# Attention's value products as one 64-column sum, with a tile of its own for minima and sums, output tiles allocated later, four buffers moved and a new instruction order

## The chip, the cores and the metric

The kernel runs on one core of a Trainium2 chip. A core has five engines that run their own instruction queues side by side: TensorE (PE, matrix products into PSUM; its weight loads are listed apart as PEld), VectorE (DVE), ScalarE (ACT), GpSimd (POOL) and SyncE (SP, which issues the DMAs here). The metric is the device time of one execution in microseconds; lower is better. Times given are medians of several runs. A profile is one further execution that was recorded.

## What is computed

One step of a decoder layer with two parallel mixers, for a prompt of 2048 tokens and for 8 x 8 sampled tokens, all in float32 at the interface:

```python
h = rmsnorm(x, norm_w)
z = h @ w_in
q, k, v, qb, kb, vb, g_lr, gate_a, gate_b = jnp.split(z, split_points(), axis=-1)
q = rope(rmsnorm(heads(q, H_A), q_norm_w), pos)
k = rope(rmsnorm(heads(k, H_A), k_norm_w), pos)
o_a = attend(q, k, v)                       # 8 heads x 64, three dilated windows
log_a = jax.nn.log_sigmoid(g_lr @ w_gate_up + b_gate) / GATE_TAU
o_b, s_fin = gla_chunked(qb * (DK_B ** -0.5), kb, vb, log_a, s0)   # 4 heads
o_b = rmsnorm(o_b, gla_norm_w)
mixed = jnp.concatenate([o_a * silu(gate_a), o_b * silu(gate_b)], axis=-1)
y = x + mixed @ w_out
```

Attention has three branches, (window, dilation) = (128, 1), (512, 4), (2048, 16). In each, a query sees at most 129 keys of its residue class:

```python
s = jnp.einsum('brnqhd,brnkhd->brnqhk', qr, kk) * (hd ** -0.5)
s = jnp.where(valid, s, -jnp.inf)
m = jnp.max(s, axis=-1, keepdims=True)
p = jnp.exp(s - m)
den = jnp.sum(p, axis=-1)
o = jnp.einsum('brnqhk,brnkhd->brnqhd', p, v) / den[..., None]
lse = m + jnp.log(den)
```

The three outputs are mixed by a softmax over their `lse`. Outputs are y, the new keys and values, and the GLA states.

## The kernel before

Products that need float32 accuracy are made from float16 halves: a number is kept as a high part and a low part, and a product is the sum of high x high, high x low and low x high. Projections (`project`, L1762) do so for each block of weights in w_in: v, q, k first, then qkb, g (in two halves g0, g1), vb and gb, tile by tile of 128 tokens. Their sums go to two PSUM banks (pool `ps_Y`), and ACT or DVE takes each out in `post`.

Attention (`attend`) works in units: 64 units of four heads for branches 1 and 2 (`unit`) and 32 half-blocks of branch 3 (`branch3`). A unit passes four steps, and units follow one another in a pipeline that is woven into the projections:

- `qk`: PE makes the scores (L1031); DVE adds the mask, scales, and takes the negated maximum as a running minimum (L1039); ACT makes the exponential and its sum (L1042). Minimum and sum go to columns 65 and 64 of the unit's output tile `o` (66 numbers a head).
- `tr`: PE transposes the probabilities (L1049), and `split` makes the two halves `pt`. Every other tile is split by ACT and DVE (L1008, L1009). The others are copied by ACT (L1011), copied once more to float16 by ACT or DVE (L1013, L1015), and the low part is POOL's subtraction (L1016). A counter decides which.
- `pv`: the value products (L1065). The values lie as [high | low], 128 columns a head. The high half of `pt` takes all 128 columns in one product, giving two sums side by side; the low half takes the 64 high columns.
- `post`: `added` has ACT copy the second sum to SBUF (`ol`, L1081) and DVE add it to the first (L1082) into `o`; a DMA writes `o` out.

The tile `o` is allocated before the scores, since minimum and sum are written to it, and is held until its DMA has read it. The outputs of the value products share two PSUM banks (`ps_O`) with GLA.

GLA works in chunks of 256 tokens (`gla_core`, `gla_prompt`), `gla_out` normalizes its output, `combine` mixes, and `finish` makes the output projection (L2121). The sampled tokens' long-range scores are multiplied on POOL (`dot`) from the cache tiles k2 and k3.

The tile framework finds the semaphores. The order in which every engine takes its instructions isn't the program's: a table `ORDER` lists, for each engine, the numbers of the traced instructions in the order wanted, and `in_order` (L675) makes each one follow its predecessor in that list. `ACT.preload_act_table_set` (L695) loads the ACT table that serves both Ln and Exp, and it too stands where the list puts it; ahead of it the compiler adds table loads of its own.

Of the kernel before, what the change touches and what calls it, by code (L numbers as in the profile page):

```python
# [7 lines left out]
F32 = mybir.dt.float32  # L8
# [10 lines left out]
P = 128  # L19
D = 1024  # L20
KT = D // P
NH = 8
# [2513 lines left out]
```

## Time and profile before

| what | value |
|---|---|
| median of 3 runs | 1230.56 us (1227.27 to 1232.08) |
| profiled execution | 1224.72 us, its span 1222.9 us |
| granted TensorE clock, mean | 0.995 |
| DVE, ACT, POOL busy | 915.3, 825.3, 540.0 us |
| value products (L1065) | 1200, 157.4 us busy |
| HBM | 183.02 MB read, 75.24 MB written |

In the rows of the profile, L and a number is a line of the kernel before. A group's row gives the engine, the operation, what it writes and reads, shapes, the count, then busy time and the mean of one in ns, then the idle time of the engine just before and what ended it. A row of the list of waits gives who waited for whom, the total in us, the times and the longest. A row of the timeline gives start and length in us; rows of one kind that follow each other are merged, with their count. The stage rows give, for each stretch, the busy time of each engine and, in brackets, its instructions, then the granted clock, the DMA engines' busy share and GB/s. A PE row's length includes the passage through the array, so neighbours overlap: the time that a product holds PE is read from start to next start.

### The profile page before, as it was taken

What the parts mean: (1) busy time and instruction counts of PE and PEld (TensorE: products, weight loads), DVE (VectorE), ACT (ScalarE), POOL (GpSimd) and SP (SyncE); (2) the same over time, 40 slices, a digit from 0 to 9 for tenths busy, and PEclk for the clock granted to TensorE, in tenths of its full rate; (3) what the DMA queues carried; (4) which work ended last, traced back from release to release, by engine and by line L of the source; (5) the groups of instructions that cost most, each with busy time, mean ns of one, the idle gap of its engine ahead of it and who ended that gap; (6) DMA issues with size and microseconds to landing.
All of it is one profiled execution on the core that took longest, in us unless ns stands there. A gap on an engine that the chain in (4) does not pass through costs nothing. (4 is left out here: it accounts for less than half of the span.)

```text
span 1222.9 us, 26121 instructions
## 1 busy us (share of the span) xinstructions
PE 1168.8 (96%) x8942; PEld 704.6 (58%) x8942; DVE 915.3 (75%) x2457; ACT 825.3 (67%) x2189; POOL 540.0 (44%) x478
## 2 busy tenths in 40 slices
PE   3999999999999889998999999999999999999998
PEld 1444465566566556665767676646556666555543
DVE  5888787978878957777778765688889999743562
ACT  7656599789779968997877563677778864521220
POOL 0054344465647335563345467655534454311220
PEclk9899999999999999999999999999999999999999
DMA  7477956777955897799999987856672287999962
GB/s 260 160 234 211 238 194 140 213 217 206 228 174 168 198 262 234 250 233 317 284 237 268 256 243 226 266 167 214 224 234 96 96 271 249 330 374 402 391 218 74
DMA packets 235831, 283.07 MB, mean 231 GB/s; under 512 B 116193, under 2 KB 146866, under 8 KB 232626
## 3 DMA queue, kind: packets, MB, share of 16 engines
q1 hardware_dynamic: 235698, 281.40, 76.1%
q8 instruction: 71, 1.16, 0.4%
q14 instruction: 62, 0.51, 0.1%
HBM read 183.02 MB, written 75.24 MB: 211 GB/s over the span
## 5 line engine op out<-in xcount | busy, mean ns | idle before, releaser
L1617 POOL TENSOR_TENSOR pr<-k,qb 128x512 f32<-128x512 f32 x128 | 169.4, 1324 | 141.9 <-DVE sck L1618 72.8
L1762 PEld LDWEIGHTS <-hr 128*128 128x128 f16 x1824 | 170.5, 98 | 103.9 <-issue 12.4
L1042 ACT ACTIVATE p<-p,o 128x256 f32<-128x256 f32 (+1 forms) x384 | 173.8, 456 | 24.3 <-DVE o L1039 16.8
L2121 PE MATMUL Y<-w_o,mh 128*128 128x512 f16 x768 | 187.7, 379 | 0.2 <-DVE xr L2128 0.2
L1762 PEld LDWEIGHTS <-hl 128*128 128x128 f16 x1248 | 117.6, 99 | 105.5 <-issue 7.5
L1065 PE MATMUL O<-v,pt 128*128 128x128 f16 (+1 forms) x1200 | 157.4, 206 | 5.6 <-POOL pt L1016 1.9
L1016 POOL TENSOR_TENSOR pt<-p,pt 128x512 f16<-128x512 f32 (+1 forms) x80 | 92.1, 1151 | 141.4 <-ACT pt L1013 88.6
L1049 PE MATMUL t<-ident,p 128*128 128x128 f32 x600 | 136.9, 282 | 4.0 <-ACT p L1042 3.5
L1065 PEld LDWEIGHTS <-pt 128*128 128x128 f16 x1200 | 100.9, 99 | 51.6 <-POOL pt L1016 7.2
L1762 PE MATMUL acc_g<-w_g,hr 128*128 128x272 f16 (+1 forms) x768 | 117.7, 276 | 0.5 <-ACT vbs L1404 0.3
L1762 PE MATMUL acc_v<-w_v,hl 128*128 128x512 f16 x384 | 113.1, 385 | 2.0 <-DVE w_v L1286 0.9
L1618 DVE TENSOR_REDUCE sck<-pr 128x8 f32<-128x512 f32 x128 | 87.2, 681 | 37.1 <-POOL pr L1617 36.7
L2121 PEld LDWEIGHTS <-mh 128*128 128x128 f16 x768 | 71.1, 98 | 69.2 <-issue 3.1
L1762 PE MATMUL acc_q<-w_q,hl 128*128 128x512 f16 x384 | 110.3, 379 | 0.0
L1762 PE MATMUL acc_k<-w_k,hl 128*128 128x512 f16 x384 | 109.4, 379 | 0.0
L1031 PE MATMUL s<-kk,qq 128*128 128x256 f16 (+1 forms) x512 | 106.2, 264 | 3.4 <-DVE o L1039 1.6
L1039 DVE CUSTOM_DVE_ANT_0 p<-s,m3w,scl_s 128x128 f32<-128x128 f32 (+1 forms) x256 | 90.7, 395 | 17.6 <-PE s L1031 8.8
L1762 PE MATMUL acc_vb<-w_vb,hr 128*128 128x512 f16 x384 | 102.1, 379 | 0.9 <-DVE so_g L1304 0.9
L1762 PE MATMUL acc_gb<-w_gb,hr 128*128 128x512 f16 x384 | 96.4, 380 | 0.1
L1049 PEld LDWEIGHTS t<-ident,p 128*128 128x128 f32 x600 | 77.9, 141 | 32.2 <-ACT p L1042 12.1
L1762 PE MATMUL acc_qkb<-w_qkb,hr 128*128 128x512 f16 x288 | 84.2, 379 | 0.0
L2163 POOL TENSOR_TENSOR oc<-oc 128x512 f32<-128x512 f32 x32 | 36.3, 1149 | 101.3 <-DVE oc L2156 86.9
(546 smaller groups left out, 2515.1 us busy)
## 6 DMA issues: line engine op xcount, KB each, us to landing
k<-in_cache_k_win SPq DMA_DIRECT2D x104, 256.0 KB
sv_b<-in_cache_v_win SPq DMA_DIRECT2D x24, 1024.0 KB
hr<-h_d SPq DMA_DIRECT2D x44, 512.0 KB
qb<-q_d SPq DMA_DIRECT2D x64, 256.0 KB
oc<-o_d SPq DMA_DIRECT2D x48, 264.0 KB
o_d<-o SPq DMA_DIRECT2D x64, 132.0 KB
x<-in_x_prompt SPq DMA_DIRECT2D x16, 512.0 KB
h_d<-hl SPq DMA_DIRECT2D x16, 512.0 KB
```

Source lines behind the costliest of these rows:

```text
L1016: POOL.tensor_tensor(l, f, h, ALU.subtract)
L1031: PE.matmul(s_ps[:, i * w : (i + 1) * w], q, k, start=(n == 0), stop=(n == len(prods) - 1),)
L1039: DVE.tensor_tensor_reduce(s[:, sl], s_ps[:, sl], mask, neg, BIG, ALU.add, ALU.min, nmf(i))
L1042: ACT.activation(s[:, sl], s[:, sl], AF.Exp, bias=nmf(i), scale=-1.0, accum_out=denf(i))
L1049: PE.transpose(p_ps[:, i * P : (i + 1) * P], t["s"][:, i * P : (i + 1) * P], ident[:])
L1065: PE.matmul(o_[:, d], t["pt"][:, c, (i * nb + b) * P : (i * nb + b + 1) * P], vf(i, b)[:, d], start=(n == 0), stop=(n == 2 * nb - 1),)
L1617: POOL.tensor_tensor(pr[:], kt, qt, ALU.mult)
L1618: DVE.tensor_reduce(out, pr[:].rearrange("p (u k d) -> p u k d", u=2, k=4), AX.X, ALU.add)
L1762: PE.matmul(z, a_[:, k, :], w[:, p_, k, cols], start=(k == 0 and i == 0), stop=(k == KT - 1 and i == 2),)
L2121: PE.matmul(Y[:], a_[:, k, :], w_[:, part, k, :512], start=(i == 0), stop=(i == len(prods) - 1),)
L2163: eng.tensor_tensor(o_[g], o_[g], w[:, g].unsqueeze(2).to_broadcast([P, NH, HD]), ALU.mult)
```

## The change

Five edits, and a new table.

1. `pv` makes, for each head and key block, three products of 64 columns, all summed in the same 64 columns of the bank: high x high, high x low, low x high. One head's output is 64 columns wide, so a unit uses 256 of a bank's 512 columns, not all.
2. `added` becomes `taken`: DVE copies the 256 columns from the bank to `o`, and ACT copies minimum and sum there from their own tile. The counter of `split` no longer jumps at an output.
3. Minima and sums go to a tile `st` of their own (six buffers), and `o` is allocated only in `post`.
4. Other homes: `gla_out` squares into `ob` rather than a tile of its own; `ct` and `tabs` are in the pool `xp`; the copy of vb is in z3 and z4 rather than z2; the cache tile k2 has two buffers.
5. `ORDER` is another table for all five engines: PE has 8619 numbers instead of 8019, DVE 2046 instead of 2014, ACT 1699 instead of 1731, POOL 474 and SP 1055 as before. Hardly a line of it is the same.

```diff
     def gla_out(gt, O, n, row0, tagp):
-        sq = gt.tile([P, 512], F32, name=f"osq_{tagp}", tag="osq")
+        ob = gt.tile([P, 512], F32, name=f"ob_{tagp}", tag="ob", bufs=2)
         ss = gt.tile([P, 4], F32, name=f"oss_{tagp}", tag="oss")
-        ACT.activation(sq[:n], O[:n], AF.Square)
-        DVE.tensor_reduce(ss[:n], sq[:n].rearrange("p (h d) -> p h d", h=4), AX.X, ALU.add)
+        ACT.activation(ob[:n], O[:n], AF.Square)
+        DVE.tensor_reduce(ss[:n], ob[:n].rearrange("p (h d) -> p h d", h=4), AX.X, ALU.add)
...
-                    for n in range(2 * nb):
-                        b, c = divmod(n, 2)
-                        d = slice(0, P - HD * c)
-                        PE.matmul(
-                            o_[:, d], t["pt"][:, c, (i * nb + b) * P : (i * nb + b + 1) * P],
-                            vf(i, b)[:, d], start=(n == 0), stop=(n == 2 * nb - 1),
-                        )
+                    for b in range(nb):
+                        for n, (c, d) in enumerate(((0, 0), (0, HD), (1, 0))):
+                            PE.matmul(
+                                o_, t["pt"][:, c, (i * nb + b) * P : (i * nb + b + 1) * P],
+                                vf(i, b)[:, d : d + HD],
+                                start=(b + n == 0), stop=(b == nb - 1 and n == 2),
+                            )
...
-        def added(out, O):
-
-            o4 = O.rearrange("p (h c d) -> p h c d", c=2, d=HD)
-            split_[0] += 2
-            l = ptp.tile([P, 4, HD], F32, name=f"ol_{split_[0]}", tag="ol", bufs=1)
-            ACT.activation(l[:], o4[:, :, 1], AF.Copy)
-            DVE.tensor_tensor(out, o4[:, :, 0], l[:], ALU.add)
+        def taken(out, O, stat):
+
+            DVE.tensor_copy(out[:, :, 0:HD], O.rearrange("p (h d) -> p h d", d=HD))
+            ACT.activation(out[:, :, HD : HD + 2], stat, AF.Copy)
...
-            ct = sm.tile([P, 2, 2, 64], F32, name=f"ct_{tag}", tag="ct", bufs=1)
+            ct = xp.tile([P, 2, 2, 64], F32, name=f"ct_{tag}", tag="ct", bufs=1)
...
-                o = zp.tile([P, 512], F32, name=f"vbs_{t}", tag="z2")
+                o = zp.tile(
+                    [P, 2, 512], F32, name=f"vbs_{t}", tag="z3" if t == "s" or t % 2 else "z4",
+                    bufs=1,
+                )[:, 0]
...
-                T["o"] = op.tile([P, 4, 66], F32, name=f"o_{br}_{m}_{pp}_{x}", tag="o")
+                T["st"] = op.tile([P, 8, 2], F32, name=f"st_{br}_{m}_{pp}_{x}", tag="st", bufs=6)
...
-                return T["O"][:, i * P : i * P + P]
+                return T["O"][:, i * HD : i * HD + HD]
...
             def post():
-                added(T["o"][:, :, 0:64], T["O"][:])
+                o = op.tile([P, 4, 66], F32, name=f"o_{br}_{m}_{pp}_{x}", tag="o")
+                taken(o, T["O"][:, : 4 * HD], T["st"][:, 0:4])
                 dst = sel((o1_d if br == 1 else o2_d)[:, oc])
-                SP.dma_start(dst, T["o"][:].rearrange("p h d -> p (h d)"))
+                SP.dma_start(dst, o[:].rearrange("p h d -> p (h d)"))
...
-                    lambda i, a=a: T["o"][:, 2 * a + i, 65:66],
-                    lambda i, a=a: T["o"][:, 2 * a + i, 64:65],
+                    lambda i, a=a: T["st"][:, 2 * a + i, 1:2],
+                    lambda i, a=a: T["st"][:, 2 * a + i, 0:1],
...
-                k2 = sk.tile([P, 512], F32, name=f"k2_{b}_{t}", tag="k2", bufs=1)
+                k2 = sk.tile([P, 512], F32, name=f"k2_{b}_{t}", tag="k2")
...
-        tabs = ap_.tile([P, 2, 2, 64], F32, name="tabs", bufs=1)
+        tabs = xp.tile([P, 2, 2, 64], F32, name="tabs", bufs=1)
```

Branch 3 is changed in the same way as `unit`. What the new table moves is shown below where it matters, in rows of the built programs' order.

More of the change, by code (lines that the diff above doesn't have):

```diff
@@ L909, in gla_out @@
     def gla_out(gt, O, n, row0, tagp):
-        sq = gt.tile([P, 512], F32, name=f"osq_{tagp}", tag="osq")
+        ob = gt.tile([P, 512], F32, name=f"ob_{tagp}", tag="ob", bufs=2)
         ss = gt.tile([P, 4], F32, name=f"oss_{tagp}", tag="oss")
-        ACT.activation(sq[:n], O[:n], AF.Square)
-        DVE.tensor_reduce(ss[:n], sq[:n].rearrange("p (h d) -> p h d", h=4), AX.X, ALU.add)
+        ACT.activation(ob[:n], O[:n], AF.Square)
+        DVE.tensor_reduce(ss[:n], ob[:n].rearrange("p (h d) -> p h d", h=4), AX.X, ALU.add)
         rs = gt.tile([P, 4], F32, name=f"ors_{tagp}", tag="ors")
         rsqrt(gt, rs[:n], ss[:n], 1.0 / 128.0, n, 4, f"o_{tagp}")
-        ob = gt.tile([P, 512], F32, name=f"ob_{tagp}", tag="ob", bufs=2)
         for h in range(4):
@@ L1579, in pre @@
                 SP.dma_start(T["v"][:], by16(vp_d[:], r))
-                T["o"] = b3.tile([P, NH, 66], F32, name=f"o3_{r}", tag="o3")
+                T["st"] = op.tile([P, 8, 2], F32, name=f"st_3_{r}", tag="st", bufs=6)
             def OT(a, i):
@@ L1584, in OT @@
                     T["O", a] = ps_O.tile([P, 512], F32, name=f"O3_{r}_{a}", tag="O")
-                return T["O", a][:, i * P : i * P + P]
+                return T["O", a][:, i * HD : i * HD + HD]
             def post(a):
-                added(
-                    T["o"][:].rearrange("p (i a) d -> p i a d", a=2)[:, :, a, 0:64], T["O", a][:]
+                if a == 0:
+                    T["o"] = b3.tile([P, NH, 66], F32, name=f"o3_{r}", tag="o3")
+                o4, st4 = (
+                    T[n_][:].rearrange("p (i a) d -> p i a d", a=2)[:, :, a] for n_ in ("o", "st")
                 )
+                taken(o4, T["O", a][:, : 4 * HD], st4)
                 if a:
@@ L1602, in branch3 @@
                     lambda i, b, a=a: T["v"][:, (2 * i + a) * P : (2 * i + a + 1) * P],
-                    lambda i, a=a: T["o"][:, 2 * i + a, 65:66],
-                    lambda i, a=a: T["o"][:, 2 * i + a, 64:65],
+                    lambda i, a=a: T["st"][:, 2 * i + a, 1:2],
+                    lambda i, a=a: T["st"][:, 2 * i + a, 0:1],
                     lambda i, a=a: OT(a, i),
```

1275 rows, old and new, of the table ORDER are left out of this document.

## The prediction

> **What bounds the kernel now.** The page comes first: TensorE (PE) against ScalarE (ACT).
>
> ```profile
> PE 1168.8 (96%) x8942; PEld 704.6 (58%) x8942; DVE 915.3 (75%) x2457; ACT 825.3 (67%) x2189; POOL 540.0 (44%) x478
> ```
>
> A busy PE need not be working at its rate, so I read the sums by stage next. Attention runs from 145 to 735 us; the first two rows are the start-up and the first projections.
>
> ```profile
> core 0: us, PE busy (x) PEld busy (x) DVE busy (x) ACT busy (x) POOL busy (x), PEclk, DMA share, GB/s
> 0.00:45.00 45.00, 24.03 (x136) 13.10 (x137) 30.55 (x70) 31.77 (x46) 2.51 (x7) 0.92 0.73 243
> 45.00:105.00 60.00, 59.14 (x275) 26.66 (x274) 47.86 (x116) 37.45 (x76) 21.60 (x25) 1.00 0.65 194
> 145.00:200.00 55.00, 52.03 (x447) 34.52 (x445) 46.13 (x167) 53.77 (x180) 21.51 (x19) 1.00 0.61 187
> 200.00:390.00 190.00, 188.14 (x1394) 118.10 (x1393) 155.81 (x414) 159.37 (x452) 108.51 (x84) 1.00 0.75 199
> 390.00:450.00 60.00, 51.79 (x387) 31.30 (x386) 44.65 (x120) 46.86 (x127) 24.17 (x17) 0.97 0.90 221
> 450.00:560.00 110.00, 108.89 (x891) 72.15 (x890) 81.59 (x262) 94.67 (x285) 61.23 (x49) 1.00 0.81 251
> 560.00:735.00 175.00, 168.98 (x1451) 120.67 (x1449) 131.14 (x425) 124.42 (x410) 81.26 (x68) 1.00 0.98 260
> ```
>
> PE leads everywhere, with two places where it stands: 21 us of the first 45, and, in the five attention rows, 590 - 569.83 = 20.2 us. ACT is the closest second there: 98% busy from 145 to 200. Third, the list of PE's waits says who ends them.
>
> ```profile
> engine line waited for: us in total, times, longest us
> PE ptx L1166 <- DVE x_s L1156: 11.6, 1, 11.6
> PE th L1136 <- ACT early_ht L1153: 5.1, 1, 5.1
> PE t L1049 <- ACT p L1042: 3.5, 8, 0.9
> ...
> PE s L1031 <- DVE o L1039: 2.9, 3, 1.4
> PE acc_v_s L1453 <- DVE w_v L1286: 2.2, 1, 2.2
> ...
> PE O L1065 <- POOL pt L1016: 1.9, 4, 0.7
> PE O L1065 <- DVE pt L1009: 1.8, 3, 1.4
> ...
> PE O L1065 <- DVE o L1082: 1.1, 1, 1.1
> PE acc_vb L1762 <- DVE so_g L1304: 0.9, 1, 0.9
> ```
>
> The chain that the change touches (scores, exponential, transpose, split into halves, value products, output) ends 3.5 + 2.9 + 1.9 + 1.8 + 1.1 = 11.2 us of PE's waits. That is all that a lighter ACT and DVE can win there directly; the rest of the kernel is PE's own work.
>
> **1. The value products.** Each of 600 (head, key block) pairs now takes three 64-column products instead of one of 128 and one of 64. This is one unit on PE before (O is the output bank, v the values, pt the transposed probabilities, acc_qkb and t other work):
>
> ```order
> L1065 LDWEIGHTS pt_2_2_1_1_0_6135
> L1065 MATMUL O_2_2_1_1_6206<-v_2_1_1_1_4112,pt_2_2_1_1_0_6135 128x128
> L1065 LDWEIGHTS pt_2_2_1_1_0_6135
> L1065 MATMUL O_2_2_1_1_6206<-v_2_1_1_1_4112,pt_2_2_1_1_0_6135 128x64
> L1762 LDWEIGHTS hl_13_3503
> L1762 MATMUL acc_qkb_13_6286<-w_qkb_5721,hl_13_3503 128x512
> ```
>
> And the same unit now:
>
> ```order
> L1120 LDWEIGHTS pt_2_2_1_1_0_6451
> L1120 MATMUL O_2_2_1_1_6526<-v_2_1_1_1_4288,pt_2_2_1_1_0_6451 128x64
> L1105 MATMUL t_2_2_1_2_0_6539<-ident_79,p_2_2_1_2_0_6458 128x128
> L1105 MATMUL t_2_2_1_2_1_6585<-ident_79,p_2_2_1_2_1_6499 128x128
> L1120 LDWEIGHTS pt_2_2_1_1_0_6451
> L1120 MATMUL O_2_2_1_1_6526<-v_2_1_1_1_4288,pt_2_2_1_1_0_6451 128x64
> ```
>
> The columns stay (192 a pair); 600 loads of weights and 600 products are added. PE's timeline has the price: start to next start.
>
> ```profile
> 300.46 0.19 PE L1065 MATMUL O<-v,pt 128*128 128x64 f16 x1
> 300.49 0.38 PE L1762 MATMUL acc_v<-w_v,hl 128*128 128x512 f16 x1
> 300.70 0.19 PE L1065 MATMUL O<-v,pt 128*128 128x64 f16 x1
> ...
> 394.69 0.79 PE L1065 MATMUL O<-v,pt 128*128 128x64 f16 x15
> 395.31 0.38 PE L1031 MATMUL s<-kk,qq 128*128 128x256 f16 x2
> ```
>
> A 64-column product holds PE for 0.03 us, one of 512 columns for 0.21: the price goes by columns. Fifteen in a row, of both widths, took 0.62 us, 41 ns each, each with its own load. So the added products cost **0** by columns; the other bound is a mean of that run for each, 600 x 41 ns = +24.6 us. I take 0, nearest to the single row. The Trainium skill, "TensorE: Matmul & The Clock Gate", section "Back-to-back issue gap", speaks against it: in a stream of load-and-product pairs a product of 128 columns takes some 81 ns. By that estimate 600 more would be +48.6 us; the trace's 41 ns for a mix of 128 and 64 disagrees.
>
> **2. ACT and DVE.** Rows by shape:
>
> ```profile
> L1082 DVE TENSOR_TENSOR o<-O,ol 128x256 f32<-128x256 f32 x96 | 40.2, 419 | 16.8 <-ACT ol L1081 16.0
> L1013 ACT ACTIVATE pt<-p 128x512 f16<-128x512 f32 x62 | 38.8, 627 | 0.4
> L1081 ACT ACTIVATE ol<-O 128x256 f32<-128x256 f32 x96 | 36.2, 377 | 21.2 <-PE O L1065 16.4 <-DVE o L1082 4.2
> L906 DVE COPY kdt_e<-ptk_e 128x512 f32<-128x512 f32 x8 | 5.5, 685 | 1.9 <-PE ptk_e L904 1.9
> L1015 DVE CAST pt<-p 128x512 f16<-128x512 f32 x8 | 5.2, 654 | 0.1
> L2151 ACT ACTIVATE oc<-oc 128x24 f32<-128x24 f32 x16 | 3.9, 246 | 29.6 <-DVE oc L2150 21.0 <-issue 6.0 <-POOL oc L2163 1.1
> ```
>
> Gone are 96 copies `ol` of 377 ns on ACT (36.2 us); in comes a copy of 8 numbers a row, whose nearest row is 24 numbers at 246 ns: 96 x 0.246 = 23.6. The counter that shares out the halves no longer jumps by two at an output, so of the 80 second copies 40 instead of 72 fall to ACT and 40 instead of 8 to DVE: 32 x 0.627 = 20.1 us off ACT, 32 x 0.654 = 20.9 onto DVE. The plain copy out of the bank costs DVE at most the 419 ns of the sum that it replaces and at least half of the 685. ACT loses 12.6 + 20.1 = 32.7 of its 479.1 us in the five stages; DVE gains 14 to 21. The bank itself is free one copy earlier: before it was read by ACT, then by DVE, which waited 16.0 us for ACT.
>
> Neither engine sets the end; the gain is what PE's waits lose. Bounds: 0 (the order refills ACT) and -20.2 us (no standing left). I take **-7**, some 60% of the 11.2 us: the waits for `p`, `POOL pt` and `o` have ACT in their chain, at 78 to 98% busy, but POOL's subtraction and DVE's minima stay. Late next is DVE.
>
> **3. Start-up.** The explicit load of the table that serves both Ln and Exp has moved. ACT's rows before, from the first scaled tile on:
>
> ```order
> L1153 ACTIVATE early_ht<-x_160 128x1024
> L695 ACT_TABLE_LOAD
> L1105 ACTIVATE jk_225,ss_188<-x_160 128x1024
> L1171 ACTIVATE hs<-ptx_251 128x4x64
> L1285 ACTIVATE w_v<-wr_v_154,ns_v 128x512
> L1142 ACTIVATE hl_190<-th_0_267 128x1024
> ```
>
> Now the same engine, a little later (rr_x is the root for the next three tiles, w_v the weights):
>
> ```order
> L1158 ACTIVATE jk_265,ss_188<-x_169 128x1024
> L1338 ACTIVATE w_v<-wr_v_165,ns_v 128x512
> L815 ACT_TABLE_LOAD
> L815 ACTIVATE rr_x_288<-rv_x_287 128x3
> L817 ACT_TABLE_LOAD
> L817 ACTIVATE rr_x_288<-rr_x_288,ln_h 128x3
> L1338 ACTIVATE w_v<-wr_v_165,ns_v 128x512
> L1161 ACTIVATE early_ht<-x_169,rs_189 128x1024
> ```
>
> Two loads now stand in that root, and two more, with the moved one, ahead of the first query tile: ten in all instead of six.
>
> ```profile
> 17.30 1.28 ACT L695 ACT_TABLE_LOAD   x1
> 18.59 1.06 ACT L1105 ACTIVATE jk<-x 128x1024 bf16<-128x1024 f32 x1
> ...
> 28.40 0.20 ACT L758 ACTIVATE rr_x<-rv_x 128x3 f32<-128x3 f32 x1 [0.23 <-DVE rv_x L757]
> ...
> 30.49 3.23 ACT L1108 ACTIVATE early_ht<-x,rs 128x1024 f16<-128x1024 f32 x3 [1.56 <-DVE rs L763]
> ```
>
> Two loads are 2.6 us; the last weight block waits behind them, and PE already stood 2.2 us for it. Of the 2.6, the load gone at 17.30 may give back up to 1.28: **+1.5** (0 to +2.6). The other three, 3.9 us, fall where ACT works 37 of 60 us and PE stands 0.9: **+0.5** (0 to +3.9). ACT's slack there hides them; without it all 3.9 would count. The Trainium skill, "ScalarE: Activation LUTs", section "What ACT_TABLE_LOAD costs", adds a drain of some 1.38 us to each switch, so the two would be 5.3 us by its estimate; the row of 17.30 is followed at 18.59, so this trace shows 1.28 alone.
>
> **4. Homes.** The vb copy leaves the two buffers that it shared with the gates (so_g).
>
> ```profile
>   DMA vb_d<-vbs: 5.1, 3
> ```
>
> That is DVE's idle time ahead of so_g until those writes had landed. PE's share of it is at most its 0.9 us wait for so_g: **-0.5** (-0.9 to 0). The square in GLA's output buffer, cos/sin tables, the cache's second buffer and `st` only change addresses: 0, hidden behind PE; if the square has to wait for its buffer's write, +1 at most by PE's longest wait of that kind (1.1 us for `o`).
>
> **5. The order.** All engines are shuffled; what I can price is how soon a projection's bank is asked for again. PE before, from the last product into acc_gb_13 to the first of acc_gb_15, which takes the same bank (sc and U are GLA's):
>
> ```order
> L1762 MATMUL acc_gb_13_13556<-w_gb_11383,hr_13_13309 128x512
> L859 MATMUL sc_e4_64_12438<-qbd0_9600,kq_e4_12117 64x128
> L1920 MATMUL U_7_12042<-vb_7_12040,kdt_e3_11949 64x128
> L859 MATMUL sc_e4_64_12438<-qbd0_9600,kq_e4_12117 64x128 x2
> L1920 MATMUL U_7_12042<-vb_7_12040,kdt_e3_11949 64x128 x2
> L859 MATMUL sc_e4_64_12438<-qbd0_9600,kq_e4_12117 64x128
> L1762 LDWEIGHTS hr_14_13388
> L1762 MATMUL acc_gb_14_13669<-w_gb_11383,hr_14_13388 128x512
> L1762 LDWEIGHTS hr_14_13388
> L1762 MATMUL acc_gb_14_13669<-w_gb_11383,hr_14_13388 128x512
> L1762 LDWEIGHTS hr_15_13483
> L1762 MATMUL acc_gb_15_13729<-w_gb_11383,hr_15_13483 128x512
> ```
>
> And now:
>
> ```order
> L1822 MATMUL acc_gb_13_14127<-w_gb_11962,hr_13_13882 128x512
> L916 MATMUL sc_e4_64_13013<-qbd0_10184,kq_e4_12692 64x128
> L1980 MATMUL U_7_12618<-vb_7_12616,kdt_e3_12526 64x128
> L916 MATMUL sc_e4_64_13013<-qbd0_10184,kq_e4_12692 64x128 x3
> L1822 LDWEIGHTS hr_15_14054
> L1822 MATMUL acc_gb_15_14300<-w_gb_11962,hr_15_14054 128x512
> ```
>
> Two products of 0.21 us have left the gap. DVE's way out of the bank:
>
> ```profile
> L1304 DVE TENSOR_SCALAR so_gb<-acc_gb,wi_gb x16: 733/745/752, 811.9 to 959.9; 128x512 f32<-128x512 f32 x16
> ```
>
> With 0.75 us to empty it, PE may stand up to 0.4 us here. Two or three such places: **+1** (0 to +10, below).
>
> **Sum.** 0 - 7 + 1.5 + 0.5 - 0.5 + 1 = **-4.5 us**. The profiled execution took 1224.72 (span 1222.9 and 1.8 around it), so 1220.2 in its terms; it was 5.8 us under the median of the runs, 1230.56, so **1226.1** as a median.
>
> **Rivals.** (a) The waits go almost whole: ACT at 98% was what stretched 145 to 200 and 390 to 450, where 11 of the 20.2 us lie. Then -16 instead of -7: 1217. Against it: the new DVE casts. (b) The change moves load without result: DVE's added 14 to 21 us take the waits over, and the start-up's +2 remain: 1232.6. (c) Slower: banks of the projections. The g, vb and gb stages have 68 tiles; where the distance falls below the emptying (0.75 us for so_gb), PE stands. At 0.15 us a tile that is +10: 1240.6 when nothing else is gained. It decides from about 0.1 us a tile on, which eats the 7. For it: the piece above; against it: so_g no longer waits for the vb writes. (d) The loads of weights don't overlap when pieces are this short: +24.6 - 4.5 = +20, 1250.7; beside it stands the page's 81 ns. Against it: the run of fifteen.
>
> **How the numbers follow.** The forecast 0.45, (a) 0.17, (b) 0.17, (c) 0.16, (d) 0.03, others 0.02. The forecast's own bounds are -10 to +1, so 0.17 of its 0.45 pass the 0.5% (6.15 us) that a measurement of this kernel can tell from no change; with (a) faster is 0.35. Slower: 0.13 of (c), (d) and others, 0.18. Same: 0.47. The range leaves out (d) and the ends: from -18.5 (all 20.2 of standing gone, start-up's +2 less the homes) to +10: 1212 to 1241.
>
> **What would show it.** Value products in a row at 28 ns and PE's matmul row unchanged but for the count: step 1; spacing of 40 ns or more: (d). ACT near 793 us plus 5 for tables, DVE near 930: step 2. PE's waits for `p`, `pt`, `o` at about 4 us: right; at 11 again: (b); near zero: (a). Ten table loads and the first 45 us with 1 to 3 us less PE: step 3. Waits of acc_g, acc_vb, acc_gb summing over 7 us: (c). I am wrong altogether if PE stands at places that I did not price, for the order was made anew everywhere.

## The result and the profile after

The changed kernel took a median of **1212.33 us** (1211.84 to 1213.26, 4 runs) against 1230.66 us for the kernel before, run beside it: ratio **0.9856**, 95% interval 0.9835 to 0.9877, so 1.44% or some 18 us faster. The two profiled executions are nearer to each other: 1213.26 us (span 1211.5) against 1224.72 (span 1222.9), 11.4 us. The trace can only explain those 11.4. The granted clock of the changed kernel's profile is no higher (0.992 against 0.995), so the clock isn't where they come from.

The page's line of engines, then the stages by the same cuts as before:

```profile
PE 1164.1 (96%) x9542; PEld 714.0 (59%) x9542; DVE 921.5 (76%) x2489; ACT 796.3 (66%) x2161; POOL 550.7 (45%) x478
```

```profile
core 0: us, PE busy (x) PEld busy (x) DVE busy (x) ACT busy (x) POOL busy (x), PEclk, DMA share, GB/s
0.00:45.00 45.00, 23.76 (x141) 12.65 (x142) 30.88 (x76) 33.13 (x48) 2.46 (x6) 0.92 0.73 244
...
145.00:200.00 55.00, 51.56 (x518) 34.94 (x517) 49.17 (x168) 50.62 (x171) 22.69 (x19) 1.00 0.65 199
200.00:390.00 190.00, 188.90 (x1604) 121.27 (x1605) 164.84 (x430) 149.71 (x440) 113.20 (x85) 1.00 0.79 201
390.00:450.00 60.00, 51.65 (x443) 33.92 (x442) 45.12 (x127) 43.96 (x129) 26.06 (x19) 0.91 0.89 222
450.00:560.00 110.00, 109.98 (x1044) 73.96 (x1041) 83.05 (x264) 84.77 (x270) 59.68 (x48) 1.00 0.84 249
560.00:735.00 175.00, 172.88 (x1595) 125.18 (x1593) 128.63 (x428) 120.11 (x415) 87.73 (x74) 1.00 1.01 267
```

ACT lost 29.0 us and DVE gained 6.2, yet in the attention rows (from 145 on) PE stands 590 - 574.97 = 15.0 us where it stood 20.2. Three quarters of the difference are in the last row (6.0 before, 2.1 now), where ACT had been least full (71%); 145 to 200, where it had been fullest (98%), and 390 to 450 stand as long as before. PE's waits:

```profile
PE th L1189 <- ACT early_ht L1206: 4.8, 1, 4.8
PE acc_qkb L1822 <- ACT zq L1435: 4.1, 1, 4.1
PE s L1087 <- DVE st L1095: 4.1, 5, 1.7
PE acc_v_s L1506 <- ACT w_v L1338: 4.0, 1, 4.0
PE u_e L867 <- ACT gT_e L864: 2.3, 2, 1.6
PE t L1105 <- ACT p L1098: 2.1, 4, 1.0
...
PE acc_vb_s L1506 <- ACT w_vb L1338: 1.1, 1, 1.1
PE acc_gb L1822 <- DVE so_gb L1357: 0.8, 1, 0.8
...
PE O L1120 <- ACT pt L1064: 0.7, 1, 0.7
...
PE O L1120 <- POOL pt L1072: 0.5, 1, 0.5
PE O L1120 <- DVE o L1134: 0.4, 1, 0.4
```

The waits for `p`, the minima, `pt` and `o` that made 11.2 us now make 2.1 + 4.1 + 0.7 + 0.5 + 0.4 = 7.8. That is 3.4 us less; no line of the profile shows where the rest of the gain is, so the experiments take the change apart.

### The profile page after: what moved, and what is told of

Read it like the earlier page. It is cut to its first block, busy times and chain, and to the rows that moved or that the text cites. A ratio compares the mean times of both kernels' runs of the same rounds, so it can differ in the third digit from the quotient of the medians.

```text
span 1211.5 us, 27234 instructions
## 1 busy us (share of the span) xinstructions
PE 1164.1 (96%) x9542; PEld 714.0 (59%) x9542; DVE 921.5 (76%) x2489; ACT 796.3 (66%) x2161; POOL 550.7 (45%) x478
## 3 DMA queue, kind: packets, MB, share of 16 engines
q8 instruction: 75, 1.23, 0.4%
## 4 chain that ended last, share of the span: by engine, by line
PE 78%; DVE 10%; ACT 6%; issue 3%; DMA 2%; POOL 1%; SPq 0%; DVEq 0%; ACTq 0%; POOLq 0%
PE Y L2181 13%; PE acc_qkb L1822 7%; PE acc_vb L1822 6%; PE acc_g L1822 6%; PE acc_v L1822 6%; PE t L1105 6%; PE s L1087 5%; PE acc_k L1822 5%; PE acc_q L1822 5%; PE acc_gb L1822 4%; PE O L1120 4%; PE OS L2438 2%; PE sc_e L932 1%; PE tm L2146 1%; PE O L1994 1%
## 5 line engine op out<-in xcount | busy, mean ns | idle before, releaser
L1822 PEld LDWEIGHTS <-hr 128*128 128x128 f16 x1824 | 167.1, 99 | 87.2 <-issue 5.1
L1120 PE MATMUL O<-v,pt 128*128 128x64 f16 x1800 | 210.7, 194 | 1.8 <-ACT pt L1064 0.7
L1098 ACT ACTIVATE p<-p,st 128x256 f32<-128x256 f32 (+1 forms) x384 | 173.3, 454 | 27.2 <-DVE st L1095 26.1
L1120 PEld LDWEIGHTS <-pt 128*128 128x128 f16 x1800 | 147.8, 101 | 61.3 <-issue 5.4
L1072 POOL TENSOR_TENSOR pt<-p,pt 128x512 f16<-128x512 f32 (+1 forms) x80 | 95.7, 1196 | 163.8 <-DVE pt L1071 72.0
L1105 PE MATMUL t<-ident,p 128*128 128x128 f32 x600 | 148.6, 289 | 2.4 <-ACT p L1098 2.1
L1822 PE MATMUL acc_g<-w_g,hr 128*128 128x272 f16 (+1 forms) x768 | 128.8, 276 | 0.0
L1087 PE MATMUL s<-kk,qq 128*128 128x256 f16 (+1 forms) x512 | 112.9, 268 | 4.2 <-DVE st L1095 4.1
L1822 PE MATMUL acc_vb<-w_vb,hr 128*128 128x512 f16 x384 | 114.4, 379 | 0.0
L1105 PEld LDWEIGHTS t<-ident,p 128*128 128x128 f32 x600 | 80.9, 142 | 25.1 <-ACT p L1098 4.1
```

The lines of the kernel that those rows point to most:

```text
L1072: POOL.tensor_tensor(l, f, h, ALU.subtract)
L1087: PE.matmul(s_ps[:, i * w : (i + 1) * w], q, k, start=(n == 0), stop=(n == len(prods) - 1),)
L1098: ACT.activation(s[:, sl], s[:, sl], AF.Exp, bias=nmf(i), scale=-1.0, accum_out=denf(i))
L1105: PE.transpose(p_ps[:, i * P : (i + 1) * P], t["s"][:, i * P : (i + 1) * P], ident[:])
L1120: PE.matmul(o_, t["pt"][:, c, (i * nb + b) * P : (i * nb + b + 1) * P], vf(i, b)[:, d : d + HD], start=(b + n == 0), stop=(b == nb - 1 and ...
L1822: PE.matmul(z, a_[:, k, :], w[:, p_, k, cols], start=(k == 0 and i == 0), stop=(k == KT - 1 and i == 2),)
```

## The experiments

Twelve kernels, each timed beside the kernel before. "Ratio" is to before, with its 95% interval; 0.001 is 1.23 us. Where an edit would not fit an order, the sequence of every engine was carried over instruction by instruction, and what only one of the kernels has was put at the time at which the trace shows its counterpart. Such an order was not fitted anew: these runs say what an order does with a program, not what the best order for that program would be.

**The yardstick: e12, the changed kernel again.** No edit.

> The changed kernel as it is, once more, since the experiments are set against it by their ratios to before, on other chips than its first runs. If those ratios can be set side by side: 0.984 to 0.987, its first ratio being 0.9856, so that e4's 0.9817 is a gain and e5, e10 and e11 are losses. If chips differ by more: outside that, and only differences over that spread count.

1216.44 us, ratio 0.9873 (0.9843 to 0.9902), just above the 0.987 that was expected at most. On this other chip the ratio moved by 0.002; smaller differences are not read, and losses and gains against the changed kernel are given from both of its ratios.

**e1, the new program in the order of before.** Its only edit beside the table puts the counter's jump back:

```diff
         def taken(out, O, stat):
+            split_[0] += 2
             DVE.tensor_copy(out[:, :, 0:HD], O.rearrange("p (h d) -> p h d", d=HD))
```

> The new program (64-column products, st, late o, the homes) with every engine's instructions in the order of before: each 128-column product is two 64-column ones at its old place, the copy of minimum and sum stands where ol stood, and the counter jumps again, so the second copies stay on ACT. Theory 1 (the lighter way out of the bank takes PE's waits away): at least half of the 18.3 us, 1222 or less. Theory 2 (the gain is the new order's, whatever the program): 1228 to 1234. If 600 more products cost PE anything, it shows here as more PE work: +3 us by the 28 ns spacing, +24 by the run of fifteen.

1220.71 us, ratio 0.9927 (0.9904 to 0.995): 9 us less than before. Theory 1 has its half, it seemed. The third question of the expectation is answered too: with 600 products more, PE's busy time is 0.5 us above the 1168.8 of before, not 3 or 24:

```profile
PE 1169.3 (96%) x9542; PEld 710.1 (58%) x9542; DVE 916.9 (75%) x2457; ACT 808.7 (66%) x2189; POOL 539.4 (44%) x478
```

**e9, the whole new program in the order of before.** The line above is out again, so DVE makes the 32 second copies.

> As e1, with the 32 second copies on DVE too, at the time at which ACT made them before: the whole new program, in the order of before. e5 put 11 us on taking these copies off ACT in the new order. If the copies are worth that in any order: 1210 to 1213 and the new order is worth nothing by itself. If they are worth it only where the order is made for it: 1218 to 1223, and the order has the rest, some 8 us.

1226.0 us, ratio 0.9973 (0.9955 to 0.9991): only 3.3 us less than before, and outside both expectations. In the old order the copies on DVE cost some 5.5 us of the 9 that e1 had won. The list of PE's waits of e9 keeps two that are GLA's and that the changed kernel lost:

```profile
PE O L1948 <- ACT ob_c L935: 3.4, 3, 1.6
...
PE sc_e L892 <- ACT qbd L851: 2.2, 3, 1.1
```

Before has the same two, of the same size:

```profile
PE O L1928 <- ACT ob_c L919: 3.4, 3, 1.6
...
PE sc_e L875 <- ACT qbd L834: 2.2, 3, 1.1
```

In the changed kernel the first is 0.3 us and the second is gone, while `zq`, `w_v` and `u_e` stand higher in its list. This is the order's work alone, for e9 and the changed kernel run the same instructions but for the four table loads that the new order brings.

**e5, the changed kernel with the second copies back on ACT,** in the new order (the same line as in e1).

> The changed kernel in its own order, but the counter jumps by two at an output again: 32 of the second copies go from DVE back to ACT, at the time at which DVE made them. e2, which put these and the bank copies back together, took 40 us more than the changed kernel. If the second copies are the cause: 1225 or more. If the bank's way out is: 1212 to 1217.

1223.45 us, ratio 0.9934 (0.9912 to 0.9956): some 8 to 10 us lost, short of the 1225 that would have made them the main cause and well over the 1217 that would have cleared them. Beside e1 (0.9927) it says more: with the second copies on ACT, the new order, as it stands and with its four more table loads, is worth nothing over the old one.

**e2, the new order with the old value products and the old way out.** The 128-column product returns, and so does ACT's copy of the second sum, here straight into `o`. The counter jumps again, so the 32 second copies are back on ACT as well; `st`, the late `o` and the new homes stay. The edit at the way out:

```diff
...
-            DVE.tensor_copy(out[:, :, 0:HD], O.rearrange("p (h d) -> p h d", d=HD))
+            o4 = O.rearrange("p (h c d) -> p h c d", c=2, d=HD)
+            split_[0] += 2
+            ACT.activation(out[:, :, 0:HD], o4[:, :, 1], AF.Copy)
+            DVE.tensor_tensor(out[:, :, 0:HD], o4[:, :, 0], out[:, :, 0:HD], ALU.add)
...
```

> The new order with the old value products (128 and 64 columns, two sums a head), ACT copying the second sum and DVE adding it, and the 32 second copies back on ACT; st, the late o and the homes stay. Theory 1: the gain falls by half or more, 1221 or more. Theory 2: it stays, 1212 to 1217.

1252.92 us, ratio 1.0189 (1.0165 to 1.0213): 23 us slower than before by its ratio, far over the 1221 that theory 1 asked for. PE's waits in e2:

```profile
PE s L1060 <- DVE st L1068: 12.3, 21, 1.9
...
PE t L1078 <- ACT p L1071: 6.3, 10, 2.0
PE O L1094 <- DVE o L1110: 5.8, 14, 1.1
```

Together 24.4 us where the changed kernel has 6.6. The new order, not fitted again, has no room for the old path; e6 and e10 ask for which part of it.

**e6 and e10: is it ACT's load, or the bank's way?** Both add 96 ACT copies of 256 columns to the changed kernel. In e6 they read the bank and DVE waits for them:

```diff
+            ACT.activation(
+                out[:, :, 0:HD], O.rearrange("p (h d) -> p h d", d=HD), AF.Copy
+            )
             DVE.tensor_copy(out[:, :, 0:HD], O.rearrange("p (h d) -> p h d", d=HD))
```

In e10 they copy `o` onto itself behind DVE, so that only the write of `o` waits:

```diff
             DVE.tensor_copy(out[:, :, 0:HD], O.rearrange("p (h d) -> p h d", d=HD))
+            ACT.activation(out[:, :, 0:HD], out[:, :, 0:HD], AF.Copy)
```

> The changed kernel in its own order with its 64-column products, and one more ACT copy of 256 columns out of the bank ahead of each of DVE's 96, which waits for it and writes the same numbers again. If the bank's longer way (ACT, then DVE) is what the new order can't bear: 1230 to 1250. If ACT's load matters only by its sum (36 of 1212 us on an engine with slack): 1212 to 1217.

> The changed kernel with 96 more ACT copies of 256 columns, as e6 has, but of the tile o onto itself behind DVE's copy, so that no bank and no product waits for them. If e6's 36 us came from ACT's load: 1235 to 1250 here too. If they came from the bank's longer way: 1212 to 1222.

e6: 1248.83 us, ratio 1.0146 (1.0122 to 1.017), 34 to 36 us slower than the changed kernel. e10: 1221.77 us, 0.9948 (0.9921 to 0.9975), 9 to 11 us slower, though its copies are no shorter. The same kind of row from both, e10's first, then the list of DVE's waits in e6:

```profile
L1138 ACT ACTIVATE o<-o 128x256 f32<-128x256 f32 x96 | 39.5, 412 | 12.9 <-DVE o L1137 12.6
```

```profile
L1137 ACT ACTIVATE o<-O 128x256 f32<-128x256 f32 x96 | 35.9, 376 | 8.6 <-PE O L1123 8.5
```

```profile
DVE o L1140 <- ACT o L1137: 69.3, 82, 9.2
```

By that, a quarter to a third of e6's loss is ACT's load; the rest goes with the place. DVE stands 69.3 us, 82 times, at the head of its queue until ACT has copied, and what is queued behind it waits too: PE's wait for the minima goes from 4.1 to 10.4 us. In before, under its own order, DVE stood 16.0 us for `ol`.

**e11, the other way: all second copies on DVE,** and the table load of e4.

```diff
-                if split_[0] % 4:
-                    ACT.activation(h, f, AF.Copy)
-                else:
-                    DVE.tensor_copy(h, f)
+                DVE.tensor_copy(h, f)
```

> e4 (one table load) with the last 40 second copies taken from ACT to DVE as well, at ACT's times. If a lighter ACT keeps paying: 1195 to 1204. If DVE is now the engine that is late: 1210 or more.

1222.23 us, ratio 0.9939 (0.9916 to 0.9963), some 15 us slower than e4. PE now waits for DVE:

```profile
PE s L1082 <- DVE st L1090: 8.0, 9, 2.6
...
PE O L1115 <- DVE o L1129: 2.7, 6, 0.7
```

So this order sits at a balance of ACT and DVE: 32 copies towards ACT cost 8 to 10 us, 40 towards DVE about 15. Some of the 15 is not DVE's work but its standing behind POOL (last section).

**e7, the price of a 64-column product.** High x low is left out of the value sums.

```diff
-                        for n, (c, d) in enumerate(((0, 0), (0, HD), (1, 0))):
+                        for n, (c, d) in enumerate(((0, 0), (1, 0))):
...
-                                start=(b + n == 0), stop=(b == nb - 1 and n == 2),
+                                start=(b + n == 0), stop=(b == nb - 1 and n == 1),
```

> The changed kernel without the product of the high half of pt and the low values (600 products and 600 loads of weights fewer; this part of the value sums is left out). If a 64-column product costs PE its 28 ns and PE sets the end: 17 us less, 1195. If 41 ns each: 25 us less, 1187. If PE's waits take the time over: 1205 or more.

1205.38 us, ratio 0.979 (0.9767 to 0.9813): 8 to 10 us less than the changed kernel, 14 to 17 ns for each product taken out, half of the 28 ns. PE's busy time fell by 12.8 us, to 1151.3, but the span only by 7.2, to 1204.3: PE stands 5.6 us longer, as the third expectation has it, and the largest growth is in its wait for the minima, from 4.1 to 6.0 us:

```profile
PE s L1053 <- DVE st L1061: 6.0, 7, 1.7
```

**e3, the home of vb alone,** in the kernel before:

```diff
-                o = zp.tile([P, 512], F32, name=f"vbs_{t}", tag="z2")
+                o = zp.tile(
+                    [P, 2, 512], F32, name=f"vbs_{t}", tag="z3" if t == "s" or t % 2 else "z4",
+                    bufs=1,
+                )[:, 0]
```

> The kernel before with one edit: the copy of vb goes to z3 and z4 and no longer shares z2 with the gates. Theory 3 (the 6.4 us that the two profiles differ by in the g and vb stage come from this home): 1224 to 1227. If the home costs nothing, as the prediction's term of -0.5: 1230 to 1231.

1227.55 us, ratio 0.9998 (0.9974 to 1.0022): nothing, in the order of before. Theory 3 is out there, although the two profiles differ most in that very stage; under the new order the home was not tried alone.

**e4 and e8: the table loads.** ACT's explicit load is number 0 in its list. In e4 it goes to the front of the changed kernel's order (and leaves its place as 62nd), in e8 to the front of before's:

```diff
     "Activation": (
-        "2-7 9 1 10 8 12 18 15 19-20 22 21 23 13 11 14 25 16-17 24 27 26 28 32 29 33-35 30-31 38 "
+        "0 2-7 9 1 10 8 12 18 15 19-20 22 21 23 13 11 14 25 16-17 24 27 26 28 32 29 33-35 30-31 "
...
```

> The changed kernel with the explicit table load as ACT's first instruction instead of its 62nd: one load is left of ten. If loads in the start-up hold PE up as the prediction priced them (+2 us for five more, of which the two in the root ahead of the last weight block count): 2 to 4 us less than the changed kernel, 1208 to 1210. If ACT's start-up lies behind the transfers of x and the weights: 1212, no change.

> The kernel before with the explicit table load as ACT's first instruction: one load instead of six, nothing else. e4 took some 5 us off the changed kernel with nine loads fewer. If before's five loads stand on the path as well: 3 to 6 us less than before, ratio 0.995 to 0.998, and the four loads that the change adds cost it 0 to 2 us. If before hides them: ratio 1.000, and the change's start-up cost it the whole 5 us.

e4: **1206.81 us** (1205.68 to 1209.61), ratio **0.9817** (0.9792 to 0.9841): it beats both kernels, the changed one by 5 to 7 us, more than the 2 to 4 expected. e8: 1226.57 us, 0.9971 (0.9951 to 0.9992), 3.6 us under before. The first 45 us of e4, then of e8:

```profile
0.00:45.00 45.00, 28.42 (x163) 15.41 (x164) 35.60 (x91) 29.73 (x49) 2.46 (x6) 0.96 0.80 265
```

```profile
0.00:45.00 45.00, 26.64 (x153) 14.13 (x154) 34.03 (x84) 26.42 (x43) 2.52 (x7) 0.96 0.76 253
```

PE is busy there for 4.66 us more than in the changed kernel (23.76; 24.22 in e12), and in e8 for 2.61 more than before (24.03). The timeline of ACT shows why; the changed kernel's first scaled tile, and e4's:

```profile
5.56 1.28 ACT L815 ACT_TABLE_LOAD   x1
6.86 0.20 ACT L815 ACTIVATE rr_xs<-rv_xs 64x1 f32<-64x1 f32 x1
7.08 1.28 ACT L817 ACT_TABLE_LOAD   x1
...
9.63 1.28 ACT L815 ACT_TABLE_LOAD   x1
...
11.30 1.28 ACT L817 ACT_TABLE_LOAD   x1
...
15.63 1.06 ACT L1206 ACTIVATE early_ht<-x 128x1024 f16<-128x1024 f32 x1
```

```profile
12.22 1.06 ACT L1204 ACTIVATE early_ht<-x 128x1024 f16<-128x1024 f32 x1
```

PE's transposes wait for that tile; it is ready 3.4 us sooner.

## Why the prediction was half right

Read side by side, the ratios make a table. Rows are programs, columns orders; the upper right kernel also has `st` with its copy, the late `o` and the new homes:

| program | order of before | new order |
|---|---|---|
| old value products, old way out | 1 | 1.0189 (e2) |
| new, second copies on ACT | 0.9927 (e1) | 0.9934 (e5) |
| new, whole | 0.9973 (e9) | 0.9856; 0.9873 (e12) |

Neither half of the change has the gain. The program alone, in the order it found, is worth 0.3%; the order alone loses 1.9%; together they win 1.3 to 1.4%. The forecast added steps up as if each had a worth of its own. Its range, 1212 to 1241, holds the measured 1212.33 by 0.3 us, and by luck: the lower end was worked out as all 20.2 us of PE's standing gone (the terms named there make -18.7, not -18.5), and 15.0 of them are still there. By its steps:

**Step 1, value products, 0: right.** PE's timeline of the changed kernel, a run of five and what follows it:

```profile
398.60 0.31 PE L1120 MATMUL O<-v,pt 128*128 128x64 f16 x5
398.74 0.31 PE L1105 MATMUL t<-ident,p 128*128 128x128 f32 x1
```

Five products hold PE for 0.14 us, 28 ns each, each with its load of weights. Over all 1800 such products of this trace the median from start to next start is 29 ns. The 41 ns that stood as the other bound was a mean of both widths, and e1's 0.5 us of PE says the same as the spacing. Rival (d) is out. The Trainium skill ("TensorE: Matmul & The Clock Gate", section "Back-to-back issue gap") states some 81 ns for such a pair with 128 columns; the pairs here, of 64 columns, stay far below it. e7 bounds what a product costs in the end: 14 to 17 ns, as PE isn't alone in setting the time.

**Step 2, ACT and DVE, -7: the durations right, the worth mis-sized.** ACT came out at 796.3 us (798 was said), DVE at 921.5 (930). The rows of the groups involved:

```profile
L1134 DVE COPY o<-O 128x256 f32<-128x256 f32 x96 | 40.2, 420 | 23.5 <-PE O L1120 23.0
...
L1135 ACT ACTIVATE o<-st 128x8 f32<-128x8 f32 x96 | 18.4, 200 | 0.0
L1071 DVE CAST pt<-p 128x512 f16<-128x512 f32 x36 | 17.2, 477 | 4.7 <-ACT p L1098 2.2 <-ACT p L1067 2.0
```

DVE's plain copy takes as long as the sum did, and the small copy 200 ns, not 246. In the old order the whole program won 3.3 us (e9), within 0 to -20.2 but half of the -7. The waits were to come down to about 4 us in the changed kernel; 7.8 are left. The forecast looked for the gain where ACT was 78 to 98% busy; PE's standing fell most in the row where ACT had been at 71%. "That is all that a lighter ACT and DVE can win there directly" was where it failed: 11.2 us of PE's waits under the old order don't tell what the same edit carries under another. In the new one, not fitted again, ACT's copy at the bank alone costs 34 to 36 us (e6).

**Step 3, start-up, +1.5 and +0.5: the price right, its sign not seen.** Ten loads as forecast. PE's wait for the last weight block (`w_v`), where the +1.5 was put, grew from 2.2 to 4.0 us. Nine loads cost the changed kernel 4.66 us of PE's first 45, five cost before 2.61: four more cost 2.05. The runs agree within their width, 5 to 7 us less 3.6. But those 45 us were to hold 1 to 3 us less of PE and lost only 0.27: with one load in each, the new order has 28.42 us of PE there (e4) against 26.64 in the old (e8), and so gives 1.78 back. What the forecast overlooked is that before had already paid for five, and that one table load would do. The Trainium skill ("ScalarE: Activation LUTs", section "What ACT_TABLE_LOAD costs") adds a drain of 1.38 us; the load at 5.56 ends at 6.84 and its successor starts at 6.86, so no run here shows it.

**Step 4, homes, -0.5:** e3's interval (-3.2 to +2.7 us) holds it and zero. The other homes were not tried alone.

**Step 5, the order, +1: wrong, and the main miss.** Rival (c) fell: PE's list of waits has 0.8 us for acc_gb and nothing from 0.2 us up for acc_g or acc_vb, not the 7 that it needed; shorter waits don't show in it, but from the first start of g's products (560.3, now 558.7) to the last of gb's (958.5, now 948.4) PE takes 8.5 us less, not more. But the step priced only what an order can lose, at one kind of place. From e9 to the changed kernel, the same instructions in another order, the ratio falls from 0.9973 to 0.9856 or 0.9873: **12 to 14 us** gained, the added table loads already paid. No term of the forecast allowed for that.

Rival (a) came nearest in time (1217), but not as a mechanism: PE's waits for the chain did not go, they fell from 11.2 to 7.8 us, and the stages that it named, 145 to 200 and 390 to 450, stand as before. The likeliest case was "within 0.5%", and it was not what happened; the sum's sign was right and its size a quarter.

**What stays open.** Between the profiled executions of e9 (span 1218.9) and of the changed kernel (1211.5) lie 7.4 us. PE's busy time has 5.6 of them, 1169.7 against 1164.1, with the same 9542 products:

```profile
PE 1169.7 (96%) x9542; PEld 709.1 (58%) x9542; DVE 928.2 (76%) x2489; ACT 795.0 (65%) x2157; POOL 542.8 (45%) x478
```

A product's row outlasts the time that it holds PE, so a short gap behind it is counted as busy: the last of the five above is 0.19 us long and holds PE for 0.03. The spacings bear this out in the main: over the six commonest shapes of product, start to next start beyond the shape's usual value (its 20th percentile), less the gaps that show between rows, sums to 43.2 us in e9 and 39.2 in the changed kernel, 4.0 of the 5.6. No single wait holds them, and what ends such a gap isn't shown. As to where, the first start into acc_g_s and the last into acc_vb and acc_gb (559.5, 798.4 and 954.8 in e9; 558.7, 795.1 and 948.4 now) put 0.8 of the 7.4 us ahead of the g stage, 2.5 in g and vb, 3.1 in gb and 1.0 behind it. And the profiled executions of before and of e9 are faster than nearly all their timed runs (e9: 1220.66 to 1229.86), while the changed kernel's is not (1211.84 to 1213.26), so that 5 us or more of the gain stand in no trace.

## What to carry to other kernels

Where a change brings a new instruction order, price program and order together: bounds from the waits under the old order hold for the old order alone, and both halves have to be run crosswise before either is given the credit. An engine at 66% can still set the time: look for the instruction at the head of another engine's queue that waits for it, not for its share. And look for the cheap thing beside the change: here it was one number in a list, an explicit table load put first, for 5 to 7 us.

## What the runs showed of the hardware

DVE's copy of 512 float32 to float16 takes 0.42 us at the median, but up to 1.49. The view by line gives the spread; the timeline of POOL and DVE shows one of the long ones:

```profile
L1071 DVE CAST pt<-p x40: 284/422/1494, 160.3 to 713.1; 128x512 f16<-128x512 f32 x36, 128x256 f16<-128x256 f32 x4
```

```profile
385.75 2.19 POOL L1677 TENSOR_TENSOR pr<-k,qb 128x512 f32<-128x512 f32 x1 [0.81 <-DVE sck L1678]
386.73 1.49 DVE L1071 CAST pt<-p 128x512 f16<-128x512 f32 x1
```

POOL's product ends at 387.94, the cast at 388.22, 0.28 us behind it, as if it had begun only then. It is no single case: each of the casts of this shape that takes over 0.45 us, 5 of 36 in the changed kernel, ends 0.28 us behind a POOL instruction that was running when it started. The same holds, at 0.28 to 0.29 us, for 3 of 8 in before, 8 of 36 in e9 and 15 of 70 in e11:

```profile
L1031 DVE CAST pt<-p x40: 283/420/1483, 159.0 to 716.5; 128x512 f16<-128x512 f32 x36, 128x256 f16<-128x256 f32 x4
```

```profile
L1066 DVE CAST pt<-p x80: 277/420/1495, 146.7 to 719.7; 128x512 f16<-128x512 f32 x70, 128x256 f16<-128x256 f32 x10
```

The Trainium skill, "SBUF — State Buffer", section "🔬 SBUF: two separate sides", says that a port pair shared by DVE and GpSimd is an exclusive lock: a GpSimd instruction, or a DVE instruction in a two-port mode, holds it to its end while the other is blocked. These rows agree, if the cast is such an instruction, which no row shows directly.

It bears on the change, since 32 such copies went to the engine that shares its port with POOL. Beyond the usual 0.42 us each, the long casts cost DVE 1.9 us in before and in e1, 4.2 in e9, 2.0 in the changed kernel and 9.3 in e11. So part of what the copies lost in e9 and e11 is this standing, and the new order meets it less often than the old one does with the same copies; what it is worth in the kernel's time was not measured.
